# Attention in pairs of steps: two score tiles, two sets of transposes, then the products of both

## Chip, cores and metric

The kernel runs on one core of a Trainium2 chip. The metric is device time in microseconds (us) of one execution, and shorter is better.

## What is computed

One layer of a decoder trunk over 2048 tokens of width 1024: an input projection, a mixer (attention and a short convolution side by side), a mixture of experts, an embedding gate and a last norm. The change touches only the attention, which has 8 heads, is causal, and runs over blocks of queries:

```
for i in range(S // Q_BLOCK):                      # 16 blocks of 128 queries
    s = q_nope . k_nope + q_rope . k_rope          # keys up to the block's end
    s = where(mask, s * scale, -inf)
    pr = softmax(s)
    outs.append(pr @ v)                            # 64 columns a head
```

## The kernel before

Everything is float32 on the outside. For TensorE each operand is split into a high part, rounded to the fp32r format, and the rest, so that a product takes two or three matmuls.

The kernel runs in stages: the projections (`project`), `attention`, `mix_out`, the experts, and `finish`. Attention is a stage of its own, between the last matmul of `project` and the first of `mix_out`.

A head's 2048 queries form 4 groups `g` of 512. A group has 4 rows `qi` of 128 queries and works on the key columns 0 to 512 (g + 1). Three lists set the order of the work, each over the same number of tiles, 4 (g + 1) for a group (4, 8, 12, 16), 40 for a head, 320 in all:

- `s_seq`: `scores(h, g, qi, c)` makes a tile of scores, 128 queries by 512 keys. TensorE does three matmuls (lines 628 to 630); on the diagonal (`c == g`) the tile is only (qi + 1) * 128 wide and a bf16 matmul adds the mask (632). VectorE takes the maximum of the tile (633), and behind a row's last tile that of the row (638). With that the row's tiles are put on the list `exps`. A score tile is one PSUM bank out of 5 (`pss`).
- `exp` is ScalarE's exponential of one score tile into `P` in SBUF, with its sum (642). It frees the bank.
- `t_seq`: `transpose(h, g, jq, qi, late)` transposes up to four 128 x 128 pieces of `P` into a bank `tr` out of 2 (`pst`, 654). `split` then copies it rounded into `pt` on ScalarE (66), and VectorE subtracts for the rest (67), which frees the bank.
- `v_seq`: `values(h, g, jq, jj)` multiplies one block of 128 keys of `pt` with the values, two matmuls into the one bank `av` (665); on the diagonal block `jj` they are 512 - 128 jj wide. Behind a group's last block `finish` copies `av` out on ScalarE (`lo`, 689), and GpSimd and DMAs do the rest.

The main loop goes over steps `n`: step `n` does `scores` of tile `n`, `transpose` of tile `n - 15` and `values` of tile `n - 22`, and takes one exponential from `exps` ahead of them. The order on each engine is the order of these calls, since the stage has a manual schedule; an instruction waits where its operands or its bank are not ready, and what stands behind it on its engine waits too. The group's last `values` call comes ahead of the step's transposes, every other one behind them.

Of the kernel before, what the change touches and what calls it, by code (L numbers as in the profile page):

```python
# [51 lines left out]
class Kernel:  # L52
# [513 lines left out]
    def attention(self, st):  # L566
# [13 lines left out]
        heads, groups, exps, qs_, undivided = {}, {}, [], {}, []  # L580

        def load_k(h, c):
            hd = heads.setdefault(h, dict(k={}, a0=64 if h % 2 else 0, b0=0 if h % 2 else 64))
            n0 = hd["a0"]
            k = hd["k"][c] = kp.tile([96, 2, 512], F32R, name="k")
            nc.sync.dma_start(k[:64].bitcast(F32), self.kd[h // 2][n0:n0 + 64, c])
            nc.sync.dma_start(k[64:].bitcast(F32), self.krd[:, c])

        def load_v(h):
            v = heads[h]["v"] = vp.tile([128, NT, 128], F32R, name="v")  # L590
            nc.sync.dma_start(v.bitcast(F32).rearrange("p t (l d) -> p t l d", l=2),
                              self.vd[:, :, h].rearrange("t p l d -> p t l d"))

        def load_q(h, g):
            q = qs_[h, g] = qp.tile([96, 2, 512], F32R, name="q")
            n0 = h % 2 * 64
            nc.sync.dma_start(q[:64].bitcast(F32), self.qd[h // 2][n0:n0 + 64, g])
            nc.sync.dma_start(q[64:].bitcast(F32), self.qrd[h // 4][h % 4, :, g])

        def scores(h, g, qi, c):  # L600

            if c == 0 and qi == 0:
                if g == 0 and h:
                    load_k(h, 2)
                    load_k(h, 3)
                if g == 3 and h + 1 < H:
                    load_k(h + 1, 0)
                    load_k(h + 1, 1)
                    load_v(h + 1)
                if hg.index((h, g)) + 2 in range(3, len(hg)):  # L610
                    load_q(*hg[hg.index((h, g)) + 2])
                G = groups[h, g] = dict(pt={}, q=qs_.pop((h, g)))
                G["P"] = [(p3 if g == 3 else p012).tile([128, (g + 1) * 512], F32, name=f"P{g}") for _ in range(4)]
                if g == 1 and R1 + h * 512 - 512 in range(R1, R2):
                    clear(R1 + h * 512 - 512)
                G["rs"] = smp.tile([128, 4, NG], F32, name="rs", bufs=3)
            G = groups[h, g]
            if c == 0:
                G["s"] = []
                G["mx"] = smp.tile([128, 5], F32, name="mx")  # L620
            mx, last = G["mx"], c == g
            w = (qi + 1) * 128 if last else 512
            s = pss.tile([128, 512], F32, name="s")[:, :w]
            G["s"].append(s)
            k = heads[h]["k"][c]
            qs = slice(qi * 128, qi * 128 + 128)
            qh, ql = G["q"][:, 0, qs], G["q"][:, 1, qs]
            mm(s, qh, k[:, 0, :w], start=True, stop=False)
            mm(s, qh, k[:, 1, :w], start=False, stop=False)
            mm(s, ql, k[:, 0, :w], start=False, stop=not last)  # L630
            if last:
                mm(s[:, w - 128:], self.identb, self.maskb, start=False, stop=True)
            nc.vector.tensor_reduce(mx[:, c:c + 1], s, axis=AX.X, op=OP.max, negate=(g == 0))  # L633
            if last:
                nm = mx[:, 0:1]
                if g:
                    nm = mx[:, 4:5]
                    nc.vector.tensor_reduce(nm, mx[:, :g + 1], axis=AX.X, op=OP.max, negate=True)
                exps.extend((G, qi, j, s, nm) for j, s in enumerate(G["s"]))

        def exp(G, qi, j, s, nm):
            nc.scalar.activation(G["P"][qi][:, j * 512:j * 512 + s.shape[1]], s, AF.Exp, bias=nm,  # L642
                                 accum_out=G["rs"][:, qi, j:j + 1])

        def transpose(h, g, jq, qi, late):
            G = groups[h, g]
            if qi == 0:
                G["pt"][jq] = tp.tile([128, 2, 4, 512], F32R, name="pt")
            pt = G["pt"][jq]
            n = 4 if jq < g else qi + 1  # L650
            ps = (pss if late % 2 else pst).tile([128, 4, 128], F32, name="tr", tag="s" if late % 2 else "tr")
            for jj in range(n):
                j = jq * 4 + jj
                nc.tensor.transpose(ps[:, jj], G["P"][qi][:, j * 128:j * 128 + 128], self.ident)  # L654
            qs = slice(qi * 128, qi * 128 + 128)
            self.split(pt[:, 0, :n, qs], pt[:, 1, :n, qs], ps[:, :n], hi_eng=nc.vector if late in (1, 3, 5) else None)

        def values(h, g, jq, jj):
            G = groups[h, g]
            j = jq * 4 + jj  # L660
            if j == 0:
                G["av"] = pso.tile([128, 512], F32, name="av")
            q0 = 0 if jq < g else jj * 128
            for hl in range(2):
                mm(G["av"][:, q0:], heads[h]["v"][:, j], G["pt"][jq][:, hl, jj, q0:], start=(j == 0 and hl == 0),  # L665
                   stop=(j == 4 * g + 3 and hl == 1))
            if j == 4 * g + 3:
                finish(h, g)
# [11 lines left out]
        def finish(h, g):  # L680

            G, a0, b0 = groups[h, g], heads[h]["a0"], heads[h]["b0"]
            av, A = G["av"], slice(a0, a0 + 64)
            lo = wk.tile([128, 512], F32, name="lo", bufs=3)
            o = wk.tile([128, 512], F32, name="o", bufs=3)
            if (h, g) == hg[-1]:
                nc.vector.tensor_copy(lo, av)
            else:
                nc.scalar.activation(lo, av, AF.Copy)
            nc.gpsimd.tensor_copy(o[A], lo[b0:b0 + 64])  # L690
            nc.gpsimd.tensor_tensor(o[A], o[A], lo[A], op=OP.add)
            normalise()
            rb = wk.tile([128, 512], F32, name="rb")
            nc.gpsimd.dma_start(rb[A], self.rd[h, g].unsqueeze(0).to_broadcast([64, 512]))
            undivided.append((h, g, o, rb, A))
            del groups[h, g]
# [8 lines left out]
        s_seq = [(h, g, qi, c) for h, g in hg for qi in range(4) for c in range(g + 1)]  # L705
        t_seq = [(h, g, jq, qi) for h, g in hg for jq in range(g + 1) for qi in range(4)]
        v_seq = [(h, g, jq, jj) for h, g in hg for jq in range(g + 1) for jj in range(4)]
        lag_t, lag_v = 15, 22
# [4 lines left out]
        def clear(r):  # L713
            nc.gpsimd.dma_start(self.yd[r:r + 512].rearrange("(p a) (b c) -> p (a b) c", p=128, c=256),
                                nought.unsqueeze(1).to_broadcast([128, 16, 256]))
# [3 lines left out]
            if g < 3:  # L719
                load_q(0, g)  # L720
        load_v(0)
        for n in range(len(s_seq) + lag_v):
            if exps:
                exp(*exps.pop(0))
            if n < len(s_seq):
                scores(*s_seq[n])
            v = v_seq[n - lag_v] if 0 <= n - lag_v < len(v_seq) else None

            ends = v is not None and v[2] == v[1] and v[3] == 3
            if ends:  # L730
                values(*v)
            if 0 <= n - lag_t < len(t_seq):
                h, g, jq, qi = t_seq[n - lag_t]
                transpose(h, g, jq, qi, max(0, n + 1 - len(s_seq)))
                if jq == g:
                    (lambda *a: None, sums, lambda *a: None, sums_row)[qi](h, g)
            if v is not None and not ends:
                values(*v)
        normalise()

# [1077 lines left out]
```

## Time and profile before

| what | value |
|---|---|
| timed runs | 2301.88, 2302.86 and 2294.78 us; median 2301.88 |
| profiled execution | 2295.84 us |
| its span, from the first to the last instruction | 2294.1 us |
| attention | 530 to 990 us of the span |
| busy in attention | TensorE 459.7 us, VectorE 386.7, ScalarE 374.5, GpSimd 160.3 |
| TensorE's granted clock | 0.989 of full over the span, 1.00 in attention |

The busy times are sums of the instructions' own durations. Matmuls overlap and their ends are modelled, so that the distance from one start to the next says how long TensorE takes, and a matmul's recorded duration is longer than that.

### The profile page before, as it was taken

The numbers are of one execution on the slowest core, as the hardware profiler recorded it, in microseconds if no ns is written. First come the engines' busy times: TensorE is split into PE (matmuls) and PEld (weight loads), VectorE is DVE, ScalarE is ACT, GpSimd is POOL, SyncE is SP. The second block draws the span as 40 slices with busy tenths as digits, with TensorE's granted clock in tenths as the row PEclk, the third lists the DMA queues.
The fourth block names the chain that finished last, engine by engine and source line by source line (L and its number), as shares of the span: only waits on it lengthen the run. The fifth ranks groups of instructions, "written<-read, shape, count | busy, mean of one in ns | idle before, by whom it ended". The sixth has DMA issues, their size and how long they took to land. (4 is left out here: it accounts for less than half of the span.)

```text
span 2294.1 us, 34784 instructions
## 1 busy us (share of the span) xinstructions
PE 2205.3 (96%) x12186; PEld 1844.3 (80%) x12186; DVE 1698.9 (74%) x3109; ACT 1324.8 (58%) x2391; POOL 503.7 (22%) x584
## 2 busy tenths in 40 slices
PE   7999999999999999999997999999999999999996
PEld 6888888888888888878885877887888888788775
DVE  6756666467888888877786778777777787777887
ACT  5433434336888888852324767667666676765443
POOL 0121201031333333320124111111111111113342
PEclk9999999999999999999998999999999999999998
DMA  7363634464453444276745779878878797873562
GB/s 234 104 225 97 221 103 154 128 208 105 127 126 84 93 103 94 45 206 212 218 163 202 274 283 362 321 260 308 325 262 295 282 352 264 310 270 125 177 200 85
DMA packets 221750, 459.36 MB, mean 200 GB/s; under 512 B 26777, under 2 KB 131266, under 8 KB 213314
## 3 DMA queue, kind: packets, MB, share of 16 engines
q1 hardware_dynamic: 178912, 333.42, 45.8%
q0 software_dynamic: 35072, 99.23, 12.6%
q10 hardware_dynamic: 7522, 23.61, 2.8%
q8 instruction: 135, 2.21, 0.4%
q14 instruction: 109, 0.89, 0.1%
HBM read 369.04 MB, written 91.33 MB: 201 GB/s over the span
## 5 line engine op out<-in xcount | busy, mean ns | idle before, releaser
L67 DVE TENSOR_TENSOR ul<-raw,uh 128x1024 fp32r<-128x1024 f32 x396 | 469.1, 1227 | 118.9 <-ACT uh L66 117.0
L66 ACT ACTIVATE uh<-raw 128x1024 fp32r<-128x1024 f32 x396 | 397.8, 1051 | 33.4 <-PE bank L76 11.2
L1390 PE MATMUL bank<-xT,uh 128*128 128x320 f32 x1024 | 275.9, 351 | 10.8 <-ACT lo L1443 8.5
L1391 PE MATMUL bank<-xT,ul 128*128 128x160 f32 x1024 | 243.4, 238 | 0.0
L67 DVE TENSOR_TENSOR pt<-tr,pt 128x512 fp32r<-128x512 f32 (+2 forms) x320 | 194.3, 609 | 59.4 <-ACT pt L66 55.9
L66 ACT ACTIVATE pt<-tr 128x512 fp32r<-128x512 f32 (+2 forms) x317 | 168.9, 533 | 74.5 <-PE tr L654 69.3
L74 PE MATMUL mm<-xh,wh 128*128 128x512 f32 x536 | 210.5, 393 | 0.0
L75 PE MATMUL mm<-xl,wh 128*128 128x512 f32 x536 | 210.2, 392 | 0.0
L76 PE MATMUL mm<-xh,wl 128*128 128x512 f32 x536 | 210.2, 392 | 0.0
L642 ACT ACTIVATE P<-s,mx 128x512 f32<-128x512 f32 (+2 forms) x320 | 198.9, 622 | 17.8 <-DVE mx L633 10.5
L1390 PEld LDWEIGHTS bank<-xT,uh 128*128 128x128 f32 x1024 | 193.4, 189 | 15.5 <-ACT lo L1443 10.0
L665 PE MATMUL av<-pt,v 128*128 128x512 f32 (+3 forms) x640 | 203.9, 402 | 0.0
L633 DVE TENSOR_REDUCE mx<-s 128x1 f32<-128x512 f32 (+2 forms) x320 | 192.2, 602 | 8.7 <-PE s L630 4.0
L1391 PEld LDWEIGHTS bank<-xT,ul 128*128 128x128 f32 x1024 | 196.8, 192 | 0.7
L66 ACT ACTIVATE wh<-raw 128x1024 fp32r<-128x1024 f32 x68 | 72.0, 1060 | 216.2 <-PE mm L75 165.3
L654 PE MATMUL tr<-ident,P 128*128 128x128 f32 x1088 | 172.8, 274 | 0.3 <-DVE pt L67 0.3
L1307 POOL DMA_DIRECT2D yd<-y x32 | 18.6, 581 | 597.6 <-ACT y L1306 597.6
L654 PEld LDWEIGHTS tr<-ident,P 128*128 128x128 f32 x1088 | 128.6, 141 | 24.0 <-DVE pt L67 1.5
L67 DVE TENSOR_TENSOR wl<-raw,wh 128x1024 fp32r<-128x1024 f32 x68 | 82.9, 1220 | 82.8 <-ACT wh L66 82.5
L74 PE MATMUL bank<-uh,xT 128*128 128x256 f32 (+1 forms) x384 | 126.3, 329 | 11.4 <-issue 10.2
L75 PE MATMUL bank<-ul,xT 128*128 128x256 f32 (+1 forms) x384 | 123.9, 323 | 4.5 <-issue 4.5
L76 PE MATMUL bank<-uh,xT 128*128 128x256 f32 (+1 forms) x384 | 124.5, 324 | 1.3 <-issue 1.3
(365 smaller groups left out, 5385.5 us busy)
## 6 DMA issues: line engine op xcount, KB each, us to landing
raw<-in_w_gate_dram SPq DMA_DIRECT2D x128, 512.0 KB, 6.8
raw<-in_w_up_dram SPq DMA_DIRECT2D x64, 1024.0 KB, 5.5
raw<-in_w_down_dram SPq DMA_DIRECT2D x128, 512.0 KB, 7.5
raw<-in_w_in_dram SPq DMA_DIRECT2D x68, 512.0 KB, 3.9
yd<-y POOLq DMA_DIRECT2D x32, 512.0 KB, 8.5
xr<-in_x_dram SPq DMA_DIRECT2D x16, 512.0 KB, 6.5
kd<-stg POOLq DMA_DIRECT2D x16, 512.0 KB, 4.0
vd<-stg POOLq DMA_DIRECT2D x16, 512.0 KB, 5.4
```

The source lines that it names most:

```text
L66: nc.scalar.activation(hi, src, AF.Copy)
L67: f = lambda: (lo_eng or nc.vector).tensor_tensor(lo, src, hi.bitcast(F32), op=OP.subtract)
L74: mm(ps, ah, bh, start=(start and i == 0), stop=False)
L75: mm(ps, ah, bl, start=False, stop=False)
L76: mm(ps, al, bh, start=False, stop=(stop and i == n - 1))
L633: nc.vector.tensor_reduce(mx[:, c:c + 1], s, axis=AX.X, op=OP.max, negate=(g == 0))
L642: nc.scalar.activation(G["P"][qi][:, j * 512:j * 512 + s.shape[1]], s, AF.Exp, bias=nm, accum_out=G["rs"][:, qi, j:j + 1])
L654: nc.tensor.transpose(ps[:, jj], G["P"][qi][:, j * 128:j * 128 + 128], self.ident)
L665: mm(G["av"][:, q0:], heads[h]["v"][:, j], G["pt"][jq][:, hl, jj, q0:], start=(j == 0 and hl == 0), stop=(j == 4 * g + 3 and hl == 1))
L1307: nc.gpsimd.dma_start(self.yd[e * 128:e * 128 + 128], y)
L1390: mm(ps[:, t, :2 * FAR], uh[:, cs], X[:, k], start=k == 0, stop=False)
L1391: mm(ps[:, t, :FAR], ul[:, cs], X[:, k, 0], start=False, stop=k == KD - 1)
```

## The change

The loop takes two steps at once. In a pair `n0`, `n0 + 1` it makes both score tiles, then both sets of transposes, then the products of both. If one of the two `values` calls is a group's last, the calls up to it come ahead of the transposes. Of the two exponentials one is called ahead of the pair, and the other between the two transposes.

```
-        for n in range(len(s_seq) + lag_v):
-            if exps:
-                exp(*exps.pop(0))
-            if n < len(s_seq):
-                scores(*s_seq[n])
-            v = v_seq[n - lag_v] if 0 <= n - lag_v < len(v_seq) else None
-
-            ends = v is not None and v[2] == v[1] and v[3] == 3
-            if ends:
-                values(*v)
+        def transposes(n):
             if 0 <= n - lag_t < len(t_seq):
                 h, g, jq, qi = t_seq[n - lag_t]
                 transpose(h, g, jq, qi, max(0, n + 1 - len(s_seq)))
                 if jq == g:
                     (lambda *a: None, sums, lambda *a: None, sums_row)[qi](h, g)
-            if v is not None and not ends:
+
+
+        for n0 in range(0, len(s_seq) + lag_v, 2):
+            if exps:
+                exp(*exps.pop(0))
+            for n in (n0, n0 + 1):
+                if n < len(s_seq):
+                    scores(*s_seq[n])
+            vs = [v_seq[n - lag_v] for n in (n0, n0 + 1) if 0 <= n - lag_v < len(v_seq)]
+
+            while any(jq == g and jj == 3 for h, g, jq, jj in vs):
+                values(*vs.pop(0))
+            transposes(n0)
+            if exps:
+                exp(*exps.pop(0))
+            transposes(n0 + 1)
+            for v in vs:
                 values(*v)
```

On TensorE, at the end of a group, the steps stood like this before; `s` are scores, `tr` transposes, `av` products, and the number behind the x is how many stand in a row:

```order
L654 MATMUL tr<-ident,P_4420 128x128 x4
L665 MATMUL av<-pt,v 128x384 x2
L628 MATMUL s<-k,q 128x512
L629 MATMUL s<-k,q 128x512
L630 MATMUL s<-k,q 128x512
L654 MATMUL tr<-ident,P_4421 128x128 x4
L665 MATMUL av<-pt,v 128x256 x2
L628 MATMUL s<-k,q 128x512
L629 MATMUL s<-k,q 128x512
L630 MATMUL s<-k,q 128x512
L665 MATMUL av<-pt,v 128x128 x2
L654 MATMUL tr<-ident,P_4422 128x128 x4
```

The same place on TensorE in the changed kernel, where the numbers of the `P` tiles are shifted by one:

```order
L628 MATMUL s<-k,q 128x512
L629 MATMUL s<-k,q 128x512
L630 MATMUL s<-k,q 128x512
L628 MATMUL s<-k,q 128x512
L629 MATMUL s<-k,q 128x512
L630 MATMUL s<-k,q 128x512
L665 MATMUL av<-pt,v 128x256 x2
L665 MATMUL av<-pt,v 128x128 x2
L654 MATMUL tr<-ident,P_4422 128x128 x4
L654 MATMUL tr<-ident,P_4423 128x128 x4
L628 MATMUL s<-k,q 128x512
L629 MATMUL s<-k,q 128x512
```

Both last products of the group now stand ahead of the two sets of transposes, and the scores of the next pair follow straight behind these.

On ScalarE, further on in the same head, the difference is this (`P` are exponentials, `pt` copies of transposed tiles):

```order
 L642 ACTIVATE P_4586,rs<-s,mx 128x256
-L66 ACTIVATE pt<-tr 128x128
+L66 ACTIVATE pt<-tr 128x4x128
 L642 ACTIVATE P_4587,rs<-s,mx 128x512
-L66 ACTIVATE pt<-tr 128x2x128
+L66 ACTIVATE pt<-tr 128x128
 L642 ACTIVATE P_4587,rs<-s,mx 128x512
-L66 ACTIVATE pt<-tr 128x3x128
+L66 ACTIVATE pt<-tr 128x2x128
```

Exponentials and copies still alternate, but each exponential stands one copy earlier than before: three tiles behind its scores and not four.

On VectorE the maxima (`mx`) and the subtractions (`pt`) alternated before:

```order
L633 TENSOR_REDUCE mx<-s 128x1
L67 TENSOR_TENSOR pt<-tr,pt 128x4x128
L633 TENSOR_REDUCE mx<-s 128x1
L638 TENSOR_REDUCE mx<-mx 128x1
L67 TENSOR_TENSOR pt<-tr,pt 128x4x128
```

In the changed kernel VectorE has them in twos:

```order
L633 TENSOR_REDUCE mx<-s 128x1 x2
L638 TENSOR_REDUCE mx<-mx 128x1
L67 TENSOR_TENSOR pt<-tr,pt 128x4x128 x2
L633 TENSOR_REDUCE mx<-s 128x1 x2
L67 TENSOR_TENSOR pt<-tr,pt 128x4x128 x2
```

A pair's two maxima now stand behind both subtractions of the pair before.

## Rows read from the trace of the kernel before

**Rows 1.** The head of the page.

```profile
span 2294.1 us, 34784 instructions
```

**Rows 2.** Windows: length, busy time of each engine, granted clock, DMA.

```profile
core 0: us, PE busy (x) PEld busy (x) DVE busy (x) ACT busy (x) POOL busy (x), PEclk, DMA share, GB/s
...
1008.40:1011.70 3.30, 3.30 (x9) 2.33 (x8) 2.23 (x4) 1.29 (x2) 0.00 (x0) 0.50 0.52 111
...
530.00:990.00 460.00, 459.70 (x2814) 381.29 (x2814) 386.74 (x805) 374.45 (x991) 160.32 (x199) 1.00 0.44 100
```

**Rows 3.** Waits, 545 to 985 us: total, times, longest.

```profile
PEld s L628 <- ACT P L642: 8.4, 31, 0.3
```

**Rows 4.** Timeline of TensorE in a plain step: start, duration, instruction.

```profile
759.67 0.39 PE L628 MATMUL s<-k,q 96*128 96x512 f32 x1
759.90 0.40 PE L629 MATMUL s<-k,q 96*128 96x512 f32 x1
...
760.38 0.60 PE L654 MATMUL tr<-ident,P 128*128 128x128 f32 x4
760.74 0.71 PE L665 MATMUL av<-pt,v 128*128 128x512 f32 x2
761.29 0.39 PE L628 MATMUL s<-k,q 96*128 96x512 f32 x1
```

**Rows 5.** Timeline of the engines at the end of a group.

```profile
774.37 0.23 PE L632 MATMUL s<-maskb,identb 128*128 128x128 bf16 x1
...
774.44 0.60 PE L654 MATMUL tr<-ident,P 128*128 128x128 f32 x4
...
775.85 0.34 PE L665 MATMUL av<-pt,v 128*128 128x128 f32 x2
...
776.03 0.62 PE L654 MATMUL tr<-ident,P 128*128 128x128 f32 x4
...
776.29 0.60 ACT L689 ACTIVATE lo<-av 128x512 f32<-128x512 f32 x1 [0.15 <-PE av L665]
...
776.78 0.59 ACT L66 ACTIVATE pt<-tr 128x512 fp32r<-128x512 f32 x1
...
777.26 0.69 ACT L642 ACTIVATE P<-s,mx 128x512 f32<-128x512 f32 x1
...
777.92 0.61 ACT L66 ACTIVATE pt<-tr 128x512 fp32r<-128x512 f32 x1
...
778.09 0.19 PEld L628 LDWEIGHTS s<-k,q 96*128 96x128 f32 x1 [0.27 <-ACT P L642]
778.10 0.49 PE L628 MATMUL s<-k,q 96*128 96x512 f32 x1
...
778.43 0.39 PE L629 MATMUL s<-k,q 96*128 96x512 f32 x1
...
778.61 0.68 DVE L67 TENSOR_TENSOR pt<-tr,pt 128x512 fp32r<-128x512 f32 x1
```

**Rows 6.** Timeline of TensorE where attention begins.

```profile
531.93 0.23 PE L632 MATMUL s<-maskb,identb 128*128 128x128 bf16 x1
531.97 0.48 PE L628 MATMUL s<-k,q 96*128 96x512 f32 x1
532.28 0.40 PE L629 MATMUL s<-k,q 96*128 96x512 f32 x1
```

**Rows 7.** Lines, 545 to 985 us: count, busy time, mean ns, idle before.

```profile
L642 ACT ACTIVATE P<-s,mx 128x512 f32<-128x512 f32 x214 | 146.7, 686 | 5.7 <-DVE mx L638 5.7
...
L66 ACT ACTIVATE pt<-tr 128x512 fp32r<-128x512 f32 x219 | 131.0, 599 | 50.7 <-PE tr L654 47.5
...
L642 ACT ACTIVATE P<-s,mx 128x384 f32<-128x384 f32 x30 | 17.5, 582 | 0.0
...
L633 DVE TENSOR_REDUCE mx<-s 128x1 f32<-128x384 f32 x30 | 16.4, 547 | 0.0
...
L66 ACT ACTIVATE pt<-tr 128x256 fp32r<-128x256 f32 x30 | 11.4, 380 | 8.0 <-PE tr L654 7.6 <-issue 0.4
```

**Rows 8.** Timeline of TensorE after attention.

```profile
1008.07 0.56 PE L74 MATMUL mm<-uh,oh 128*128 128x512 f32 x1 [2.53 <-ACT oh L66]
```

## The prediction

> **What bounds the kernel now.** I read the page first, then the stretch of the changed code by windows, then the waits, then two stretches of the timeline. The profiled execution took 2295.84 us, 1.7 us more than its span [rows 1]; the three timed runs have a median of 2301.88, so this one lies near the fastest of them. Attention is the stretch from 530 to 990 us: there TensorE is busy for 459.7 of 460 us at a granted clock of 1.00, while VectorE is busy for 387 and ScalarE for 374 [rows 2]. TensorE's busy time alone proves little, because the ends of matmuls are modelled. The distances between starts prove more. In a plain step three score matmuls take 0.71 us (759.67 to 760.38), four transposes 0.36 until the first product starts, and two products 0.55, together 1.62 us [rows 4]. At 0.235 us for a matmul of 512 columns (759.67 to 759.90) and 0.11 us for a transpose, that is what five matmuls and four transposes take one behind the other (1.61). So TensorE runs nearly without a gap. The one wait of weight loads that comes back is that of the first score matmul for an exponential, 31 times [rows 3]; each costs TensorE 0.10 us, since the matmul behind such a late load holds the array for 0.33 us in place of 0.23 (778.10 to 778.43) [rows 5].
>
> **What keeps these waits short.** A score tile takes the PSUM bank of the tile five before it, and that bank is free when its exponential is done. ScalarE works in order, and the exponential stands behind the copies of transposed tiles. Rows 5 show the longest form of this chain, at the end of a group. Count from the first of the two last products, which are 128 wide (775.85): the transposes start 0.18 later, the copy `lo` of the finished sum 0.44, the copy of the transposed tile (`pt`) 0.93, the exponential 1.41, and the load that waited for it 2.24 (778.09). In that time TensorE had transposes, scores, transposes and products to do, so the wait was short.
>
> **The change, part by part.** The number of matmuls, copies and reductions stays; only the order changes. A pair holds scores, scores, transposes, transposes, products, products, and ScalarE has exponential, copy, exponential, copy.
>
> *Switches saved.* The transposes pass over after only 0.03 us of their last 0.11, and the first product then takes 0.32 instead of 0.235 (two take 0.55 and not 0.47) [rows 4]. The two cancel, so a switch costs between 0 and 0.085 us; I take 0.01 us a step from the sum above (1.62 against 1.61). Half of 320 steps: -1.6 us.
>
> *Masks.* Where the tile on the diagonal is the first of a pair, the mask's bf16 matmul is now followed by score matmuls and not by transposes. At the start of attention, where this already happens, the mask takes 0.04 and the next matmul 0.31 [rows 6]; before transposes it takes 0.07 (774.37 to 774.44) [rows 5], and the later matmul 0.235. That is 0.045 us more. Diagonals at tiles 0 and 2 of group 0 and 14 and 20 in group 2: 4 a head, 32 in all, +1.4 us.
>
> *Plain pairs.* The exponential in the middle of a pair frees the bank of the second score tile of the next pair. From the start of the first transposes to that tile's first matmul, the chain is 0.60 (transposes [rows 4]), 0.48 (copy, 776.78 to 777.26), 0.83 (exponential to load, 777.26 to 778.09) and 0.10 for the open load [rows 5]: 2.01 us. TensorE has two sets of transposes (0.87), four product matmuls (0.94) and one score tile (0.71) before it: 2.52 us. No wait, with 0.5 us to spare; all the cover is in the products.
>
> *Ends of groups.* There the two last products, 256 and 128 wide, come before the transposes. A group has 4, 8, 12 or 16 tiles and the products lag by 22 steps, so the end is always the second of a pair, and the pair has no product behind its transposes. Count as before: the load comes at 2.24, and with 0.10 for the open load the tile starts in effect at 2.34. TensorE is there at 0.18 + 0.44 + 0.44 + 0.71 = 1.77: a wait of **0.57 us** where before it was 0.10. Of the 32 ends 30 have scores behind them. Fifteen have these sizes. In the eight ends of group 0 the transposes are two and three (0.33 us less cover) and the copy is 256 wide, 380 ns in place of 599 [rows 7]: 0.57 + 0.33 - 0.22 = 0.68. In the seven ends of group 2 the exponential is 384 wide, 582 ns in place of 686: 0.47. Sum: 15 x 0.57 + 8 x 0.68 + 7 x 0.47 = **17.3 us**.
>
> In these sums the open load counts 0.10 us, since load and matmul begin together where the load waited (778.09 and 778.10) [rows 5]. The Trainium skill ("TensorE: Matmul & The Clock Gate", Part 3, The mechanism) says that TensorE, out of a queue of 64, pulls a weight load ahead of running matmuls where the two do not conflict. By that the wait alone would count, and the 17.3 us would be 30 x 0.10 = 3.0 us less; the row decides here, because the load itself carries the wait.
>
> *What is late next.* The second copy stands behind the middle exponential, at 1.41 + 0.66 (777.26 to 777.92); VectorE's subtraction follows 0.69 later (778.61) and takes 0.68 [rows 5]; with 0.1 for the hand-over, as long as from the exponential's end (777.97) to its load, its transpose bank is free at 3.54. TensorE comes back for it, two sets on, at 2.34 + score tile + 0.44. For a score tile of 384 with mask (0.60, eight places, behind group 1) that is 3.38, a wait of 0.16; for one of 256 (0.42, seven places, behind group 2, all 0.10 earlier) 3.10 against 3.44, 0.34; for a full tile nearly none. 8 x 0.16 + 7 x 0.34 = 3.7 us. Behind group 1, too, the maxima of both tiles stand on VectorE behind that subtraction: from 2.76, 0.60 for it, 0.60 and 0.55 for the two maxima (the second 384 wide, 547 ns [rows 7]), 0.2 for the row's maximum and hand-overs, so the row's first exponential starts at 4.71 and frees its bank at 5.64; TensorE has, from 2.34, 0.60 + 0.44 + 0.16 + 0.11 + 0.94 + 0.71 and is there at 5.30. 0.34 us, eight times: 2.7 us.
>
> *Sum.* 17.3 + 3.7 + 2.7 = 23.7 us of new waits, less 31 x 0.10 = 3.1 that they replace, less 1.6, plus 1.4: +20.4 us, so 2295.84 + 20.4 = 2316.2. In the first 22 steps there are no products to cover anything; that may add 1 us. As the runs' median lies 6 us above the profiled execution, I forecast **2318 us**, its own range 2309 to 2326.
>
> VectorE and ScalarE keep some 70 us of slack in the stage, so they do not become the bound by their sums. The loads on SP and the small transfers on POOL are issued with the same tiles, at most one step earlier or later, and no row of TensorE waits for either in this stage.
>
> **The rivals.**
> *The slack hides it (no change).* VectorE and ScalarE are idle for 16 and 19% of the stage, and the exponentials stand one copy earlier than before. If the chains start early enough to take up the 0.57 us, only the small terms remain: 2295.84 - 3.1 - 1.6 + 1.4 = 2292.5. Against it: idle time before the end does not help a chain that starts at the last product. The Trainium skill ("Perfetto Trace Analysis", Identifying the Most-Contended Engine) says that the engine with the highest occupancy is the one that limits, and takes busy share as a fair measure for ScalarE and VectorE. By that neither would limit here and the time would be that of this rival; the stage before agrees, its waits were 3.1 us. 0.11.
>
> *Switches are dear (faster).* If the 0.085 us of the first product behind transposes is not given back by the 0.03 hand-over, 160 switches fewer save 13.6 us, and without new waits the time is 2295.84 - 13.6 - 3.1 + 1.4 = 2280.5. It decides if eight transposes in a row take clearly under 0.8 us to the first product. The sum of 1.61 speaks against it. 0.04.
>
> *Every pair waits (slower still).* If ScalarE runs late by more than the 0.5 us to spare, each of the 130 or so full pairs waits, by 0.2 us say, and 26 us come on top: 2344. It speaks against it that ScalarE has 2.3 us of work (two copies of 0.48, two exponentials of 0.66) in a pair of 3.2. 0.03.
>
> *The clock falls.* It was 0.50 of full, the lower level of 1.2 GHz, from 1008.4 on [rows 2], after TensorE had been idle for 2.53 us [rows 8]. New gaps of 0.7 us are far shorter, and the stage with its transposes in every step had 1.00 throughout. At the lower level a matmul took 0.37 us (3.30 us by nine), so each fall costs some 1.2 us; at all 30 ends 36 us, 2354. 0.02.
>
> **How the numbers follow.** 0.80 for the forecast. The range 2304 to 2327 holds the forecast's own range and reaches down to where only the 17.3 us, shortened by half, are left (2301 + some of the 6 us between runs) and up to the further 1 us of the start, all waits a tenth longer, and the slower of the runs. From no change a measurement here can tell about 0.5%, 11 us. Slower 0.80: nearly all of the forecast's 0.80 but 0.05, plus 0.05 of the two slower rivals. Within 0.5%: 0.11 + 0.05 = 0.16. Faster: 0.04.
>
> **What would show it.** In the profile after: waits of the score loads for `P` some 40 times, long ones of about half a microsecond in the second tile behind each group's end; TensorE no longer whole in every slice of attention; the stage some 20 us longer, and all that follows only shifted. Two sets of transposes should start the first product about 0.8 us after their own start. The mask's cost shows between two score tiles. The prediction is wrong if `pt` and `P` follow the last product sooner than 0.93 and 1.41 us, or if the plain pairs wait.

## The result, and the profile after

The change makes the kernel slower, by 0.8%. Six runs of it have a median of 2316.23 us (2311.81 to 2321.79), six of the kernel before 2297.94 (2294.08 to 2302.86). The ratio is 1.0077, with a 95% interval from 1.0064 to 1.0090. The forecast was 2318 us, from terms that added up to 20.4 us more.

The profiled execution of the changed kernel took 2314.20 us, 18.4 more than the one before. Its page begins so ([rows 1]):

```profile
span 2312.5 us, 34784 instructions
```

Windows say where the 18.4 us lie. The columns are the stretch, its length, the busy time of each engine with its instructions, the granted clock, and the DMA. First the kernel before, attention and all that follows it:

```profile
529.70:990.30 460.60, 460.30 (x2818) 381.86 (x2816) 386.84 (x805) 374.75 (x992) 160.32 (x199) 1.00 0.44 100
...
990.30:2294.00 1303.70, 1228.00 (x6995) 1034.90 (x6994) 990.89 (x1732) 745.62 (x1079) 256.59 (x211) 0.98 0.71 251
```

And the same two stretches of the changed kernel:

```profile
530.70:1011.60 480.90, 469.71 (x2818) 386.30 (x2816) 386.34 (x805) 366.39 (x992) 160.07 (x199) 1.00 0.44 99
...
1011.60:2312.00 1300.40, 1225.05 (x6996) 1033.54 (x6995) 991.51 (x1732) 745.03 (x1080) 258.80 (x211) 0.98 0.71 251
```

Attention is 20.3 us longer, with the same instructions: what is new is waiting. Of the 20.3, 10.9 show as idle time of TensorE (0.3 before, 11.2 after) and 9.4 as busy time, because a matmul is recorded as longer (0.39 us) than the 0.23 from its start to the next one's, and so hides the first part of each wait; the tables below go by starts. The stretch ahead of attention is 1.0 us longer and the rest is 3.3 us shorter, although nothing in either was changed; the last section comes back to the rest.

The view of the waits of the changed kernel, 545 to 1003 us (total, times, longest), beside the one wait of [rows 3], which covers the like stretch of the kernel before:

```profile
PEld s L628 <- ACT P L642: 27.5, 40, 0.9
...
PE s L628 <- ACT P L642: 9.9, 32, 0.4
...
PEld tr L654 <- DVE pt L67: 2.5, 9, 0.3
```

The load of a score tile now waits 27.5 us for exponentials where it waited 8.4, and for the first time the matmuls themselves show such a wait. All but two of the 40 are the 30 ends of groups and the eight places, one a head, where a row's maximum is late behind group 1. The timeline of the changed kernel at the end of a group 0, to be read against [rows 5]:

```profile
792.76 0.59 PE L665 MATMUL av<-pt,v 128*128 128x256 f32 x4
...
793.18 0.73 PE L654 MATMUL tr<-ident,P 128*128 128x128 f32 x5
793.44 0.60 ACT L689 ACTIVATE lo<-av 128x512 f32<-128x512 f32 x1 [0.81 <-PE av L665]
...
793.93 0.38 ACT L66 ACTIVATE pt<-tr 128x256 fp32r<-128x256 f32 x1
...
794.20 0.69 ACT L642 ACTIVATE P<-s,mx 128x512 f32<-128x512 f32 x1
794.22 0.39 PE L630 MATMUL s<-k,q 96*128 96x512 f32 x1
...
794.77 0.21 ACT L642 ACTIVATION_READ_ACCUMULATOR P<-s,mx 128x1 f32 x1
...
795.03 0.19 PEld L628 LDWEIGHTS s<-k,q 96*128 96x128 f32 x1 [0.86 <-ACT P L642]
795.03 0.33 PE L628 MATMUL s<-k,q 96*128 96x128 f32 x1 [0.43 <-ACT P L642]
...
795.20 0.28 PE L629 MATMUL s<-k,q 96*128 96x128 f32 x1
...
795.50 1.17 PE L654 MATMUL tr<-ident,P 128*128 128x128 f32 x8
```

The four products of the end are over, and ScalarE goes `lo`, copy, exponential, and the read of the exponential's sum, which ends at 794.98. The load follows 0.05 us later. In that time TensorE has five transposes and one score tile. The last matmul of this tile starts at 794.22, and the next tile's first not 0.23 later but 0.81: 0.58 of waiting. It also holds the array 0.17 us (795.03 to 795.20), where the first matmul of a tile of this width takes 0.06 with its load ahead (787.95 to 788.01 in the kernel with only the scores in pairs, below): 0.11 more, together 0.69.

The other three ends of a head, and the place behind group 1 where the row's maximum is late, in the timeline of TensorE; each time the last matmul of the first tile and the first two of the second, with the transposes behind groups 1 and 2 and, at 756.92, those of the first pair of a head:

```profile
756.92 1.19 PE L654 MATMUL tr<-ident,P 128*128 128x128 f32 x8
...
788.42 0.39 PE L630 MATMUL s<-k,q 96*128 96x512 f32 x1
789.12 0.50 PE L628 MATMUL s<-k,q 96*128 96x512 f32 x1 [0.32 <-ACT P L642]
789.46 0.39 PE L629 MATMUL s<-k,q 96*128 96x512 f32 x1
...
806.62 0.40 PE L630 MATMUL s<-k,q 96*128 96x512 f32 x1
807.32 0.44 PE L628 MATMUL s<-k,q 96*128 96x384 f32 x1 [0.31 <-ACT P L642]
807.60 0.34 PE L629 MATMUL s<-k,q 96*128 96x384 f32 x1
...
808.02 0.84 PE L654 MATMUL tr<-ident,P 128*128 128x128 f32 x5
...
810.11 0.39 PE L630 MATMUL s<-k,q 96*128 96x512 f32 x1
810.60 0.50 PE L628 MATMUL s<-k,q 96*128 96x512 f32 x1
810.93 0.40 PE L629 MATMUL s<-k,q 96*128 96x512 f32 x1
...
824.94 0.39 PE L630 MATMUL s<-k,q 96*128 96x512 f32 x1
825.54 0.39 PE L628 MATMUL s<-k,q 96*128 96x256 f32 x1 [0.21 <-ACT P L642]
825.76 0.28 PE L629 MATMUL s<-k,q 96*128 96x256 f32 x1
...
826.06 1.34 PE L654 MATMUL tr<-ident,P 128*128 128x128 f32 x8
```

From these rows, with 0.23 us taken off the first distance and the matmul's own 0.23, 0.17 or 0.12 (512, 384 or 256 wide) off the second:

| place | wait predicted | wait measured |
|---|---|---|
| end of group 0 (794.22) | 0.68 | 0.58 + 0.11 = 0.69 |
| end of group 1 (806.62) | 0.57 | 0.47 + 0.11 = 0.58 |
| end of group 2 (824.94) | 0.47 | 0.37 + 0.10 = 0.47 |
| end of group 3 (788.42) | 0.57 | 0.47 + 0.11 = 0.58 |
| late row maximum behind group 1 (810.11) | 0.34 | 0.26 + 0.10 = 0.36 |
| transposes behind group 1 (808.02) | 0.16 | 0.84 - 0.71 = 0.13 |
| transposes behind group 2 (826.06) | 0.34 | 1.34 - 1.04 = 0.30 |
| transposes behind group 0 (795.50) | none | 1.17 - 1.04 = 0.13 |
| transposes in the first pair of a head (756.92) | none | 1.19 - 1.04 = 0.15 |

The 0.71 and 1.04 are what five and eight transposes take where no bank is waited for, at 780.92 and 778.09 in the kernel with all products behind the transposes (next section). The places repeat in the other heads with the same sizes to some hundredths; in the first head some are shorter.

### The profile page after: what moved, and what is told of

Its sections match the earlier page's. It is cut to its first block, busy times and chain, and to the rows that moved or that the text cites. A ratio compares the mean times of both kernels' runs of the same rounds, so it can differ in the third digit from the quotient of the medians.

```text
span 2312.5 us, 34784 instructions
## 1 busy us (share of the span) xinstructions
PE 2211.8 (96%) x12186; PEld 1847.4 (80%) x12186; DVE 1699.1 (73%) x3109; ACT 1315.5 (57%) x2391; POOL 506.0 (22%) x584
## 5 line engine op out<-in xcount | busy, mean ns | idle before, releaser
L67 DVE TENSOR_TENSOR ul<-raw,uh 128x1024 fp32r<-128x1024 f32 x396 | 469.6, 1230 | 117.9 <-ACT uh L66 117.6
L642 ACT ACTIVATE P<-s,mx 128x512 f32<-128x512 f32 (+2 forms) x320 | 200.9, 628 | 18.3 <-DVE mx L633 10.5
L633 DVE TENSOR_REDUCE mx<-s 128x1 f32<-128x512 f32 (+2 forms) x320 | 183.9, 603 | 3.6 <-PE s L630 1.8
L665 PE MATMUL av<-pt,v 128*128 128x512 f32 (+3 forms) x640 | 165.4, 381 | 0.0
L654 PE MATMUL tr<-ident,P 128*128 128x128 f32 x1088 | 150.8, 275 | 0.6
L74 PE MATMUL bank<-uh,xT 128*128 128x256 f32 (+1 forms) x384 | 126.4, 329 | 12.3 <-issue 10.9
L628 PE MATMUL s<-k,q 96*128 96x512 f32 (+2 forms) x320 | 125.5, 392 | 10.6 <-ACT P L642 9.9
L654 PEld LDWEIGHTS tr<-ident,P 128*128 128x128 f32 x1088 | 119.7, 141 | 11.8 <-DVE pt L67 2.5
```

The costliest lines, as they stand in the source:

```text
L67: f = lambda: (lo_eng or nc.vector).tensor_tensor(lo, src, hi.bitcast(F32), op=OP.subtract)
L74: mm(ps, ah, bh, start=(start and i == 0), stop=False)
```

## Experiments

Three theories were held against each other. A is the prediction's: the products that stand ahead of the transposes leave the chain from copy to exponential to score bank without cover. B: pairs as such cost, since copies and maxima come in twos. C: the copy `lo` in ScalarE's queue costs. Each ratio is to the kernel before, timed again beside the runs (medians 2299.55 us for the first, second, third and fourth experiment, 2300.72 for the others).

### All products behind the transposes

```
-            while any(jq == g and jj == 3 for h, g, jq, jj in vs):
-                values(*vs.pop(0))
```

> The changed kernel, but at a group's end too all products stand behind the two sets of transposes. Theory A (the products ahead of the transposes leave the chain from copy to exponential to score bank without cover): the chain of 2.01 us from the first transposes now has 0.87 + 0.35 (products 256 and 128 wide) + 0.71 = 1.93 us beside it, and the copy lo comes behind both copies, so the 30 waits of 0.47 to 0.68 fall to 0.1 and below: about 2316 - 16 = 2300 us, 2296 to 2304. Theory B (the pairs themselves are the cost: maxima and copies in twos come late, wherever the products stand): 2311 us or more. Theory C (the copy lo in ScalarE's queue is the cost): also about 2300, since lo leaves the chain; the run with lo on VectorE tells A from C.

Measured: 2303.15 us, ratio 1.0019 (1.0009 to 1.0028). By the ratios three quarters of the loss are gone with two lines; by the stage's own window it is 17.8 of 20.3 us, with attention at 463.1 in place of 480.9:

```profile
530.90:994.00 463.10, 461.88 (x2818) 386.61 (x2816) 385.45 (x805) 363.52 (x992) 160.29 (x199) 1.00 0.45 99
```

An end of a group 3 in this kernel's timeline, with the five transposes of the pair behind it, and further on the place behind group 1 where a row's maximum is late:

```profile
778.09 1.04 PE L654 MATMUL tr<-ident,P 128*128 128x128 f32 x8
...
778.88 0.65 PE L665 MATMUL av<-pt,v 128*128 128x256 f32 x4
...
779.89 0.40 PE L630 MATMUL s<-k,q 96*128 96x512 f32 x1
780.04 0.19 PEld L628 LDWEIGHTS s<-k,q 96*128 96x128 f32 x1 [0.20 <-ACT P L642]
780.12 0.42 PE L628 MATMUL s<-k,q 96*128 96x512 f32 x1
...
780.92 0.71 PE L654 MATMUL tr<-ident,P 128*128 128x128 f32 x5
...
799.77 0.40 PE L630 MATMUL s<-k,q 96*128 96x512 f32 x1
800.26 0.50 PE L628 MATMUL s<-k,q 96*128 96x512 f32 x1
```

The load is still late, but the tile starts 0.23 us after the one before it (779.89 to 780.12), so TensorE hardly waits. This refutes B as the cause of the loss: the pairs are all still there. A small part of B is true. The late row maximum, which the prediction worked out from two maxima in a row, costs the same 0.26 as before from start to start (799.77 to 800.26, less 0.23), and the stage is still 2.5 us longer than in the kernel before. The eight transposes pass over to the first product after 0.79 us.

### Single steps, all products behind the transposes

```
-            ends = v is not None and v[2] == v[1] and v[3] == 3
+            ends = False
```

> The kernel before, single steps, but a group's last product too stands behind its transposes. Theory A: the early product is no evil in itself; in single steps it lets lo start ahead of the copy, and a score tile or a product stands behind the transposes anyway. Moved behind, lo starts some 0.4 us later, between the copy and the next exponential, so each of 31 ends waits 0.1 to 0.3 us more: 2301 to 2306 us beside 2298 before. Theory B and C: no change or a small gain, 2294 to 2299.

Measured: 2304.24 us, ratio 1.0023 (1.0011 to 1.0034), attention 464.9 us. So the same edit that wins 17.8 us of the stage in pairs loses 4.3 in single steps. The loads of score tiles wait 11.7 us for exponentials here, where they waited 8.4 before. What counts is not where the products stand but what stands beside the chain.

```profile
530.40:995.30 464.90, 463.95 (x2818) 381.21 (x2816) 388.91 (x805) 375.68 (x991) 160.21 (x199) 1.00 0.44 100
```

### The changed kernel with `lo` on VectorE

```
-            if (h, g) == hg[-1]:
+            if True:
                 nc.vector.tensor_copy(lo, av)
```

> The changed kernel with lo, the copy of the finished sum, on VectorE for every group (ScalarE had it in 31 of 32). Theory A: the copy of the transposed tile can then start with the end of the transposes, 0.80 after the last product began and not 0.93, so 0.1 us less at 30 ends (-4 us), while VectorE has 0.69 us more at each end, of which up to 0.1 shows: 2311 to 2317 us. Theory C: the half microsecond of lo leaves the chain, 30 x 0.5 = 15 us: 2301 us.

Measured: 2318.56 us, ratio 1.0089 (1.0070 to 1.0107), not told apart from the change itself. Its attention is 3.7 us shorter, and the rest was 7.7 longer in this execution:

```profile
531.70:1008.90 477.20, 469.93 (x2818) 386.36 (x2817) 402.76 (x836) 351.19 (x961) 160.02 (x199) 1.00 0.45 99
1008.90:2317.00 1308.10, 1227.22 (x6996) 1035.54 (x6995) 991.32 (x1732) 745.54 (x1080) 259.14 (x211) 0.98 0.71 249
```

The 3.7 us are about the 4 that A gave; C wanted 15. They are spread otherwise than A had it: behind groups 1 to 3 the waits are 0.09 us shorter, behind group 0 it is 0.30 (from the first tile's last matmul to the second tile 793.21 to 793.72, where it was 794.22 to 795.03). The median lies 1.6 us above the expected range; in the profiled execution it is the part behind attention that is longer, and for the other runs this is not shown.

### Only the scores in pairs

Behind the two score tiles, transposes and products go step by step, a group's last product ahead of its own transposes:

```
-            vs = [v_seq[n - lag_v] for n in (n0, n0 + 1) if 0 <= n - lag_v < len(v_seq)]
-            while any(jq == g and jj == 3 for h, g, jq, jj in vs):
-                values(*vs.pop(0))
-            transposes(n0)
-            if exps:
-                exp(*exps.pop(0))
-            transposes(n0 + 1)
-            for v in vs:
-                values(*v)
+            for n in (n0, n0 + 1):
+                if n > n0 and exps:
+                    exp(*exps.pop(0))
+                v = v_seq[n - lag_v] if 0 <= n - lag_v < len(v_seq) else None
+                ends = v is not None and v[2] == v[1] and v[3] == 3
+                if ends:
+                    values(*v)
+                transposes(n)
+                if v is not None and not ends:
+                    values(*v)
```

> Only the two score tiles are in a pair; behind them transposes and products go step by step as in the kernel before (transposes, products, transposes, products; a group's last product ahead of its own transposes). Theory A: at an end one of the two last products and one set of transposes stand behind the first set, so most of the chain has cover; but the second score tile still needs the exponential behind the first copy: half of the waits stay, 2305 to 2312 us. Theory B, if the two score tiles in a row are the cost: 2314 to 2318; if the two sets of transposes are: 2297 to 2300.

Measured: 2306.30 us, ratio 1.0038 (1.0025 to 1.0051); attention takes 470.4 us. About half of the loss stays, within the range that A gave, but not for A's reason. An end of a group 0, and the place behind group 1 where the row's maximum is late:

```profile
787.72 0.40 PE L630 MATMUL s<-k,q 96*128 96x512 f32 x1
787.95 0.22 PE L628 MATMUL s<-k,q 96*128 96x128 f32 x1
788.01 0.27 PE L629 MATMUL s<-k,q 96*128 96x128 f32 x1
...
802.64 0.40 PE L630 MATMUL s<-k,q 96*128 96x512 f32 x1
802.77 0.69 ACT L642 ACTIVATE P<-s,mx 128x512 f32<-128x512 f32 x1 [0.99 <-DVE mx L638]
...
803.60 0.51 PE L628 MATMUL s<-k,q 96*128 96x512 f32 x1 [0.56 <-ACT P L642]
```

At this end the second tile starts 0.23 us behind the first one's last matmul, and at the other ends of the head the tile loses 0.05 at most: the waits of score tiles that were to stay by half are gone. What stays is the late row maximum, 0.96 less 0.23 and with 0.10 for the open load 0.83 us, where the changed kernel has 0.36; in eight heads that is 6.6 of the 9.8 us that the stage is longer than before. So the hit was luck, and here the two score tiles in a row, the first form of B, are what costs most, though far less than B said (2314 to 2318). Why the maximum comes later here than in the changed kernel was not followed. The waits of this kernel, 545 us to the end of attention and a little beyond, show one more place:

```profile
PEld s L628 <- ACT P L642: 15.6, 33, 1.0
...
PEld tr L654 <- DVE pt L67: 11.9, 36, 0.5
```

Transposes wait for their own bank 36 times, where the changed kernel has nine such waits.

### Both exponentials ahead of the pair

```
-            if exps:
-                exp(*exps.pop(0))
+            for _ in range(min(2, len(exps))):
+                exp(*exps.pop(0))
...
             transposes(n0)
-            if exps:
-                exp(*exps.pop(0))
             transposes(n0 + 1)
```

> The changed kernel, but both exponentials of a pair are called ahead of it, none between the transposes. Theory A: the exponential that frees the second score tile's bank now stands behind the second copy. From the second transposes the chain is again 2.01 us, with 0.44 + 0.94 + 0.71 = 2.09 beside it in a plain pair (even), but only 0.44 + 0.71 = 1.15 at a group's end: waits of 0.9 us in place of 0.57 at 30 ends, and some at plain pairs: 2326 to 2338 us. If ScalarE's order does not matter (a rival of A): 2314 to 2318.

Measured: 2332.29 us, ratio 1.0135 (1.0121 to 1.0150), attention 498.7 us. An end of a group 1:

```profile
820.21 0.40 PE L630 MATMUL s<-k,q 96*128 96x512 f32 x1
...
821.39 0.44 PE L628 MATMUL s<-k,q 96*128 96x384 f32 x1 [0.79 <-ACT P L642]
```

From start to start it is 1.18 us, a wait of 0.95 and with the open load 1.05, where the chain behind the second copy gave 0.9 and the changed kernel has 0.58. ScalarE's order decides.

### Pairs shifted by one step

```
-        for n0 in range(0, len(s_seq) + lag_v, 2):
+        for n0 in range(-1, len(s_seq) + lag_v, 2):
...
-                if n < len(s_seq):
+                if 0 <= n < len(s_seq):
```

> The changed kernel with the pairs shifted by one step, so that a pair is an odd step and the even one behind it. The group's end is then the first of a pair, and the second product stays behind the transposes. Theory A in its simple form (only the products at the end matter) would have the waits at the ends gone: about 2300 us. Theory A with the whole chain: rows of four tiles in group 3 now end on the first score tile of a pair, so the row's first exponential must wait for a maximum that is ready only after the pair's scores, and the next pair's first score tile needs the bank that it frees, with no score tile beside the chain as cover: about 0.9 us in most pairs of groups 2 and 3, 100 pairs or so: 2380 to 2420 us. Theory B (pairs as such): 2316.

Measured: 2406.20 us, ratio 1.0461 (1.0446 to 1.0477), attention 571.0 us. The simple form of A falls here: the products at the ends are not all. The waits of this kernel:

```profile
PEld s L628 <- ACT P L642: 127.9, 272, 0.9
```

Nearly every score tile waits, 272 loads and not the 100 pairs that I had expected, for shorter times each; the total came out in the range although count and size did not, so this hit is in part luck. The order of the calls says why it is not only rows of four. A pair has two tiles and two calls for an exponential. With the shift, the call ahead of the pair in which the first row of four ends finds the list empty; nothing makes that call up, and from then on every score tile needs an exponential that stands one call later than in the changed kernel. So a pair must be laid so that a row of four tiles ends on its second tile; that this alone would do it is not shown.

### Two score tiles, then transposes and products in turn

```
-            while any(jq == g and jj == 3 for h, g, jq, jj in vs):
-                values(*vs.pop(0))
             transposes(n0)
             if exps:
                 exp(*exps.pop(0))
+            if vs:
+                values(*vs.pop(0))
             transposes(n0 + 1)
```

With this all products stand behind their transposes.

> Two score tiles, transposes, products, transposes, products, with a group's last product behind the transposes like every other. Theory A: as in the run with all products behind, and the products between give the second bank of transposes more time: 2296 to 2303 us, no more than 2 us from that run. Theory B (two sets of transposes or two score tiles in a row are the cost): half way between, 2305 to 2310.

Measured: 2302.94 us, ratio 1.0009 (0.9999 to 1.0019), attention 462.4 us, 0.7 less than with all products behind. No version beats the kernel before, and pairs have little to win: its own waits and switches were some 5 us of 2296.

## Why the prediction was right

**Plain pairs, and ends of groups.** The step that carried the sum held place by place (table above), and moving the products back took away what it had given to the ends.

**What is late next.** The late row maximum came as worked out, 0.36 for 0.34. So did the waits of the transposes at the two places of the sum, 0.13 for 0.16 and 0.30 for 0.34; but the sum left out two more places in a head, 0.13 behind group 0 and 0.15 in its first pair, so that this term is about 5 us and not 3.7 (8 x 0.13 + 7 x 0.30 + 8 x 0.13 + 7 x 0.15 = 5.2).

**The waits replaced.** The 31 x 0.10 = 3.1 us counted only the open load. In the kernel before some of these tiles also started late; set against the usual distances, the starts of all its matmuls in attention give about 5 us for late score tiles (an estimate), and 21.7 in the changed kernel. The difference of 16.7 is near the 17.3 + 2.7 - 3.1 = 16.9 of the terms, though both parts of it are larger. The stage grew by 20.3 us where the terms gave 20.4: errors of one or two us cancel, and the agreement to a tenth is luck.

**Switches.** Eight transposes in a row take 0.79 us to the first product (778.09 to 778.88), seven times 0.11 and the 0.03 of the hand-over, and so not clearly under the 0.8 us that dear switches would have shown. That the small term, -1.6 us, was won is not shown by itself.

**Masks.** Where a mask is followed by scores, it is still the 0.04 and 0.31 of [rows 6]: 777.28, 777.32 and 777.63 in the kernel with all products behind:

```profile
777.28 0.23 PE L632 MATMUL s<-maskb,identb 128*128 128x128 bf16 x1
...
777.32 0.47 PE L628 MATMUL s<-k,q 96*128 96x512 f32 x1
...
777.63 0.39 PE L629 MATMUL s<-k,q 96*128 96x512 f32 x1
```

**The open load.** The 0.10 us that the first matmul takes longer behind a load that waited was there at every place, and the hundredths by which the loads follow the read of the sum are in the 0.83 from exponential to load.

**The rivals.** Slack did not hide the wait: VectorE and ScalarE are idle for 20 and 24% of the stage and TensorE waits for them all the same, since the chain starts late, not slowly. Switches were not dear, plain pairs did not wait, and the clock stayed at 1.00 through attention.

**The level.** The forecast stood 2 us above the sum of 2316.2 because the first three runs had a median 6 us above the profiled execution; with three more that distance is 2 us, and the median came out at the sum. That it did so to a tenth is luck too: the medians are 18.3 us apart and not 20.4.

## What to carry over

Work that a chain needs beside it must stand behind the chain's start on the engine that will wait; to batch like with like moves it, so lay out the chain with the durations of the old trace at every irregular place (group ends, short rows), not in the plain step alone. A busy share of 80% says nothing about such a chain. Which position of a batch a row ends on can cost more than the batching can win: 571 against 481 us for the stage by one step of shift.

## What was not expected of the hardware

The part behind attention, untouched by any of these kernels, took 1299.4 to 1308.3 us in the nine traces of this case (1303.7, 1300.4 and 1308.1 in the windows above), at a granted clock of 0.98 or 0.99. One difference can be seen. In the kernel before the clock was at the lower level, 0.50, from 1008.4 to 1011.7 us [rows 2], 18 us behind attention; in the changed kernel no such fall came there, and a window from the end of attention to 1230 us has 1.00. The five traces with a fall within 20 us behind attention have 1301.8 to 1308.3 us for the part, the four without one 1299.4 to 1302.7. But one fall costs only some 1.2 us, by the prediction's estimate, and the kernel before and the one with `lo` on VectorE both have this fall and are 4.4 us apart. So most of the spread of 9 us stays open. A difference of a few us between single executions is therefore best read from the stage's own window.
